# The first RMSNorm's mean square from squares of the transposed x, added on VectorE and summed by matmuls, in one encoder layer on one core

## The chip, the cores and the metric

The kernel runs on one core of a Trainium2 chip. The metric is the device time of one execution in microseconds (us), lower is better; the runs of the kernel before are summed up by their median. Engines are named as in the profile: PE is TensorE's matmul, PEld its weight load, DVE VectorE, ACT ScalarE, POOL GpSimd, SP the engine whose queue issues the loads (SPq).

## The reference, cut to what matters

One layer over x of 256 positions (T) by 2048 channels (D). Only the first lines concern the change; the rest is three branches and an MLP, all large matmuls.

```python
def rms_norm(x, g):
    y = xf * lax.rsqrt(jnp.mean(xf * xf, axis=-1, keepdims=True) + NORM_EPS)
    return y.astype(x.dtype) * g

h = rms_norm(x, norm1_g[i])
proj = h @ w_in[i]     # columns: z | xBC | dt | q | k | v | GLU | gates
dt = jax.nn.softplus(dt_raw + dt_bias)
q = rms_norm(q, q_g); k = rms_norm(k, k_g)
...
x = x + merged @ w_out[i]
x = x + relu(rms_norm(x) @ w_up)^2 @ w_down
```

## The kernel before

**Blocks and units.** All large products run as a list of blocks, each of up to 512 output columns; a block is cut into units of 256 rows of the contraction. For unit k the kernel loads a slab of weights (`raw`, line 1193, five buffers), splits it into a rounded part `hi` on ACT (line 1211) and a remainder `lo` on DVE (line 255), four buffers each, and PE does twelve (or 24 narrower) matmuls: `hi` with the activation's rounded part (1273, or 1264), `hi` with its remainder (1274, 1266), `lo` with the rounded part (1276, 1268). A block of mode "X" sums into a PSUM tile `main`, of which there are two, used in turn.

**The first blocks.** Block 0 holds the columns of dt and of the first queries (448 columns, units 0 to 7), block 1 the first keys (384 columns, units 8 to 15), block 2 the first values (384 columns, units 16 to 23). They use the unnormed x times g1 (`xgh`, `xgl`, lines 307 and 308; x is loaded transposed into four slabs `xt`, channel on the partition), and each position's factor 1/rms is multiplied in afterwards. From block 3 (unit 24, the first GLU block) on, the activation is the normed h, as `hh` and `hl`.

**The jobs around the change.** `job_rms1` finds that factor. It loads x again in natural layout (position on the partition, four `xr` of 512 KB), takes sums of squares on ACT, gets the factor per partition `r` (`st["r1"]`) from `rstd_steps`, and `spread` brings it into a row that stands on every partition, `rbc`, by a matmul of a diagonal `dg` with ones (line 296). `job_h` waits for `rbc` and makes h: sixteen `hf` on DVE (354), four `hh` on ACT (357), four `hl` on DVE (255). `job_dt` waits for `r`, reads block 0's dt columns into `dtt` (386), permutes them by matmuls (395), and computes a softplus on ACT and DVE (399 to 424), then `adt` and four matmuls with masks (436). `job_qk` (one for the queries, one for the keys) takes squares of a block on ACT (459), makes the factor `qrs` on DVE, scales into `qn` on ACT (489), marks its `main` as free, and transposes `qn` on PE (501) into `qkT` (505, 506).

**What sets the order.** Each engine works through its instructions in the order in which the Python program writes them. A planner (class `Sched`) steps the jobs, which are generators: they ask for an estimated time on an engine ("v", "a", "g", "p"), for slabs ("m"), banks ("b"), a delay ("w") or a condition ("j"), and are taken forward between units as long as the planner's credit and its own clock allow. Jobs have a priority (0 for `job_rms1` and `job_qk`, 1 for `job_h` and `job_dt`). For unit k the program writes the split of unit k + 3, then the matmuls of unit k. Where a unit needs something that no job has written yet, `require` writes the jobs' steps at once, whatever they cost: first those of priority 0, then those of 1, in the order in which they were added. The first unit of block 2 needs the PSUM tile of block 0:

```python
if u == 0:
    if bi >= 2:
        j = mains[bi - 2]
        S.require(lambda: id(j) in st["main_free"], f"block {bi - 2} read")
...
# require: while not cond(): the jobs with prio <= level, forced
for j in [x for x in self.jobs if x.prio <= level]:
    while not cond() and not j.done and self._try(j, True):
        moved = True
# job_qk of block 0, before it marks the tile as free
if off:
    yield "j", lambda: "dt_read" in st
st["main_free"].add(id(main))
```

Of the kernel before, what the change touches and what calls it, by code (L numbers as in the profile page):

```python
# [15 lines left out]
AF = mybir.ActivationFunctionType  # L16
ALU = mybir.AluOpType
AX = mybir.AxisListType
# [3 lines left out]
T = 256  # L22
D = 2048
KC = D // P
HEADS = 32
EPS = 1e-6
# [164 lines left out]
def kernel(ctx: ExitStack, tc: tile.TileContext, xT, xn, par, cm, cd, cq, w1, wq, ws, out):  # L191
    nc = tc.nc
    S = Sched()
# [11 lines left out]
    def nm(s):  # L205
        cnt[0] += 1
        return f"{s}_{cnt[0]}"

    def slab(shape, dt=F32, name="s"):
        return gp.tile([P] + list(shape), dt, tag="g", name=nm(name))  # L210

    def bank(shape=(512,), name="b"):
        return pd.tile([P] + list(shape), F32, tag="d", name=nm(name))

    def small(shape, name, dt=F32, bufs=None):
        return sm.tile([P] + list(shape), dt, tag=name, name=nm(name), bufs=bufs)

    V, A, G, PE = nc.vector, nc.scalar, nc.gpsimd, nc.tensor
# [6 lines left out]
    xt = []  # L225
# [11 lines left out]
    onesd = cp.tile([P, P], F32, name="onesd")  # L237
# [9 lines left out]
    def natural(ap):  # L247

        return ap.rearrange("p (j r) -> p r j", r=2)

    def strided(ap):
        return ap.rearrange("p (r j) -> p r j", r=2)
# [12 lines left out]
    def rstd_steps(dst, ms, n):  # L265

        s = small([n], f"rs{n}", bufs=2 if n < 64 else 1)
        r = small([n], f"rr{n}", bufs=2 if n < 64 else 1)
        yield "a", 1500 + n
        A.activation(s, ms, AF.Sqrt)  # L270
        yield "w", 1
        yield "v", (100 if n == T else 800) + 7 * n
        V.reciprocal(r, s)
        for b_ in (r, ms):
            if n == T:
                yield "v", 200 + n
            V.tensor_tensor(s, r if b_ is r else s, b_, op=ALU.mult)
        if n == T:
            yield "v", 200 + n
        V.tensor_scalar(s, s, -0.5, 1.5, op0=ALU.mult, op1=ALU.add)  # L280
        if n == T:
            yield "v", 200 + n
        V.tensor_tensor(dst, r, s, op=ALU.mult)

    def spread(r):

        yield "m", 1
        dg = slab([2, P], name="dg")
        yield "v", 400
        for t in range(2):  # L290
            V.tensor_scalar(dg[:, t, :], ID, r[:, t:t + 1], None, op0=ALU.mult)
        yield "w", 1
        yield "b", 1
        b = bank()
        yield "p", 440
        PE.matmul(b[:, :T], ones, dg, start=True, stop=True)
        S.give()
        yield "w", 1
        return b[:, :T]
# [9 lines left out]

    def job_rms1():  # L310

        xss = small([2, 2], "xss1", bufs=1)
        yield "m", 4
        xs_ = []
        for t in range(2):
            for e in range(2):
                xr = slab([1024], name="xr")
                nc.sync.dma_start(xr, xn.rearrange("(p t) d -> p t d", t=2)[:, t, e * 1024:e * 1024 + 1024])
                xs_.append(xr)
        yield "w", 2  # L320
        for t in range(2):
            for e in range(2):
                yield "a", 1300
                xr = xs_[2 * t + e]
                A.activation(xr, xr, AF.Square, accum_out=xss[:, t, e:e + 1])
        S.give(4)
        yield "w", 1
        m2 = small([2], "ms2", bufs=2)
        yield "v", 300
        V.tensor_reduce(m2, xss, axis=AX.X, op=ALU.add)  # L330
        V.tensor_scalar(m2, m2, 1.0 / D, EPS, op0=ALU.mult, op1=ALU.add)
        r2 = cp.tile([P, 2], F32, name="r2")
        yield from rstd_steps(r2, m2, 2)
        st["r1"] = r2
        b = yield from spread(r2)
        rbc = small([T], "rbc", bufs=1)
        yield "v", 400
        V.tensor_copy(natural(rbc), strided(b))
        S.banks += 1
        st["rbc1"] = rbc  # L340

    def job_h():
# [758 lines left out]
    def start_jobs():  # L1101
        S.add(job_rms1(), "rms1", 0)
# [61 lines left out]
    for o in ORDER:  # L1164
        k, i = o[0], int(o[1])
# [235 lines left out]
```

## Time and profile before

| | |
|---|---|
| median of 3 runs | 1981.73 us (1981.35 to 1984.19) |
| profiled execution, device time | 1983.86 us |
| its span, first to last instruction | 1982.1 us |
| PE busy | 1966.0 us, 99% |
| DVE busy, ACT busy, POOL busy | 1309.0, 1036.0, 47.5 us |
| read from HBM | 360.45 MB |

Start times in the rows below are microseconds from the span's start. A row of the timeline gives start, duration, engine, line, operation, output and inputs, and in brackets how long the engine had been idle and what ended that. A row of the groups gives line, engine, operation, shapes and count, then busy time and the mean ns of one. Instructions of one engine overlap a little at their ends, so that a chain of them is shorter than the sum of their durations. A matmul of plain fp32 data appears as two records.

### The profile page before, as it was taken

The numbers are of one execution on the slowest core, as the hardware profiler recorded it, in microseconds if no ns is written. First come the engines' busy times: TensorE is split into PE (matmuls) and PEld (weight loads), VectorE is DVE, ScalarE is ACT, GpSimd is POOL, SyncE is SP. The second block draws the span as 40 slices with busy tenths as digits, with TensorE's granted clock in tenths as the row PEclk, the third lists the DMA queues.
The fourth block names the chain that finished last, engine by engine and source line by source line (L and its number), as shares of the span: only waits on it lengthen the run. The fifth ranks groups of instructions, "written<-read, shape, count | busy, mean of one in ns | idle before, by whom it ended". The sixth has DMA issues, their size and how long they took to land.

```text
span 1982.1 us, 29949 instructions
## 1 busy us (share of the span) xinstructions
PE 1966.0 (99%) x11798; PEld 1766.0 (89%) x11798; DVE 1309.0 (66%) x1847; ACT 1036.0 (52%) x1446; POOL 47.5 (2%) x42
## 2 busy tenths in 40 slices
PE   8999999999999999999999999999999999999999
PEld 7999999999998888888888888999988998998887
DVE  5778887887887889896654555555555554455443
ACT  6654576777757655545654444544443443344332
POOL 0000010000000000003000000000000000000000
PEclk9999999999999999999999999999999999999999
DMA  8555554554554555555555556555555555555554
GB/s 284 184 175 183 165 185 145 167 172 144 184 170 161 176 181 178 183 191 187 190 191 183 189 189 207 194 186 192 188 190 189 189 191 191 188 186 191 190 181 149
DMA packets 105342, 364.51 MB, mean 184 GB/s; under 512 B 11760, under 2 KB 12272, under 8 KB 105200
## 3 DMA queue, kind: packets, MB, share of 16 engines
q1 hardware_dynamic: 103904, 360.23, 55.4%
q10 hardware_dynamic: 1296, 2.36, 0.3%
q8 instruction: 92, 1.51, 0.3%
q14 instruction: 50, 0.41, 0.1%
HBM read 360.45 MB, written 2.10 MB: 183 GB/s over the span
## 4 chain that ended last, share of the span: by engine, by line
PE 95%; DVE 0%; issue 0%
PE main L1273 19%; PE main L1274 19%; PE main L1276 19%; PE main L1266 11%; PE main L1264 11%; PE main L1268 11%; PE b L842 1%; PE b L864 1%; PE b L968 1%; PE b L1273 0%; PE b L1274 0%; PE b L1276 0%; PE b L819 0%; PE b L501 0%; PE b L757 0%; PE b L742 0%
## 5 line engine op out<-in xcount | busy, mean ns | idle before, releaser
L255 DVE TENSOR_TENSOR lo<-raw,hi 128x1024 fp32r<-128x1024 f32 (+2 forms) x697 | 831.5, 1194 | 643.5 <-ACT hi L1211 638.7
L1211 ACT ACTIVATE hi<-raw 128x1024 fp32r<-128x1024 f32 (+2 forms) x695 | 716.2, 1032 | 868.7 <-PE main L1274 487.8
L1273 PE MATMUL main<-hi,hh 128*128 128x512 f32 (+1 forms) x800 | 306.1, 383 | 0.0
L1274 PE MATMUL main<-hi,hl 128*128 128x512 f32 (+1 forms) x800 | 299.0, 374 | 0.0
L1266 PE MATMUL main<-x2l,hi 128*128 128x256 f32 x1024 | 246.4, 281 | 0.0
L1264 PE MATMUL main<-x2h,hi 128*128 128x256 f32 x1024 | 246.3, 279 | 0.0
L1266 PE MATMUL main<-hl,hi 128*128 128x256 f32 x896 | 216.3, 281 | 3.2 <-DVE hl L255 3.2
L1264 PE MATMUL main<-hh,hi 128*128 128x256 f32 x896 | 217.7, 282 | 0.0
L565 DVE SCALAR_TENSOR_TENSOR co<-cin,cpar,co 128x256 f32<-128x256 f32 x480 | 211.1, 491 | 0.0
L1276 PE MATMUL main<-lo,hh 128*128 128x512 f32 (+1 forms) x800 | 200.5, 372 | 0.0
L1264 PEld LDWEIGHTS main<-x2h,hi 128*128 128x128 f32 x1024 | 192.7, 188 | 0.2
L1266 PEld LDWEIGHTS main<-x2l,hi 128*128 128x128 f32 x1024 | 192.6, 188 | 0.2
L1273 PE MATMUL main<-hi,ah 128*128 128x512 f32 x480 | 188.9, 394 | 0.0
L1274 PE MATMUL main<-hi,al 128*128 128x512 f32 x480 | 188.6, 393 | 0.0
L1273 PEld LDWEIGHTS main<-hi,hh 128*128 128x128 f32 x800 | 152.5, 191 | 23.4 <-ACT hi L1211 1.2
L1274 PEld LDWEIGHTS main<-hi,hl 128*128 128x128 f32 x800 | 152.2, 190 | 22.9 <-issue 1.9
L1266 PEld LDWEIGHTS main<-hl,hi 128*128 128x128 f32 x896 | 168.8, 188 | 4.2 <-DVE hl L255 3.6
L1264 PEld LDWEIGHTS main<-hh,hi 128*128 128x128 f32 x896 | 169.2, 189 | 0.6
L1276 PEld LDWEIGHTS main<-lo,hh 128*128 128x128 f32 x800 | 148.0, 190 | 22.1
L1268 PE MATMUL main<-x2h,lo 128*128 128x256 f32 x1024 | 138.3, 277 | 0.0
L1276 PE MATMUL main<-lo,ah 128*128 128x512 f32 x480 | 130.1, 393 | 0.0
L1268 PEld LDWEIGHTS main<-x2h,lo 128*128 128x128 f32 x1024 | 127.6, 188 | 0.0
(244 smaller groups left out, 2304.5 us busy)
## 6 DMA issues: line engine op xcount, KB each, us to landing
raw<-ws_dram SPq DMA_DIRECT2D x600, 512.0 KB, 3.3
raw<-wq_dram SPq DMA_DIRECT2D x88, 384.0 KB, 3.1
raw<-w_dram SPq DMA_DIRECT2D x7, 448.0 KB, 7.0
xr<-xn_dram SPq DMA_DIRECT2D x4, 512.0 KB, 9.2
x<-xn_dram SPq DMA_DIRECT2D x4, 512.0 KB, 4.3
xt<-xT_dram SPq DMA_DIRECT2D x7, 256.0 KB, 7.0
out_dram<-x SPq DMA_DIRECT2D x4, 256.0 KB, 3.7
out_dram<-x ACTq DMA_DIRECT2D x4, 256.0 KB, 5.6
```

What stands on the lines that cost most here:

```text
L255: V.tensor_tensor(lo, raw, hi.bitcast(F32), op=ALU.subtract)
L565: V.scalar_tensor_tensor(dst[:, e, :], x[:, e, k:k + T], par_("dw", (2 * i + e) * 31 + k), dst[:, e, :], op0=ALU.mult, op1=ALU.add)
L842: PE.matmul(ba, lt, src, start=(n == 0), stop=(n == 3))
L864: PE.matmul(bd[:, i, :], em[:, 0, i, :], x[:, c, pr:pr + P], start=True, stop=True)
L968: PE.transpose(b[:, e, t * P:t * P + P], src[:, t, k * P:k * P + P], ID)
L1211: A.activation(h, r, AF.Copy)
L1264: PE.matmul(o, wh[:, e, cs], ah, start=(first and e == 0 and c % 2 == 0), stop=False, skip_group_check=True)
L1266: PE.matmul(o, wh[:, e, cs], al, start=False, stop=False, skip_group_check=True)
L1268: PE.matmul(o, wl[:, e, cs], ah, start=False, stop=(last and e == 1), skip_group_check=True)
L1273: PE.matmul(o, ah[:, xs_], wh[:, e, :], start=(first and e == 0), stop=False)
L1274: PE.matmul(o, al[:, xs_], wh[:, e, :], start=False, stop=False)
L1276: PE.matmul(o, ah[:, xs_], wl[:, e, :], start=False, stop=(last and e == 1))
```

## The change

`job_rms1` no longer loads x a second time. It squares the four slabs `xt` on ACT (into `xacc` and, three times, into one slab `xsq`), adds them on DVE (three additions of 128x1024, then one of 128x512 and one of 128x256), and sums over the partitions by matmuls with a matrix of 1/D: two of two columns, which give the mean square per partition, and one of 256 columns, which gives it as a row on every partition. Both go through `rstd_steps`, the second with 256 columns; `spread` and the copy into `rbc` fall away.

```diff
     def job_rms1():
-        xss = small([2, 2], "xss1", bufs=1)
-        yield "m", 4
...
-                nc.sync.dma_start(xr, xn.rearrange("(p t) d -> p t d", t=2)[:, t, e * 1024:e * 1024 + 1024])
...
-                yield "a", 1300
-                A.activation(xr, xr, AF.Square, accum_out=xss[:, t, e:e + 1])
+        yield "m", 2
+        acc = slab([4, T], name="xacc")
+        sq = slab([4, T], name="xsq")
+        for i in range(4):
+            yield "a", 1050
+            A.activation(sq if i else acc, xt[i], AF.Square)
+            yield "w", 1
+            if i:
+                yield "v", 1200
+                V.tensor_tensor(acc, acc, sq, op=ALU.add)
+        yield "v", 620
+        V.tensor_tensor(acc[:, 0:2, :], acc[:, 0:2, :], acc[:, 2:4, :], op=ALU.add)
+        yield "v", 350
+        V.tensor_tensor(acc[:, 0, :], acc[:, 0, :], acc[:, 1, :], op=ALU.add)
+        yield "w", 1
+        yield "b", 1
+        b = bank()
+        yield "p", 900
+        for t in range(2):
+            PE.matmul(b[:, T + 2 * t:T + 2 * t + 2], acc[:, 0, t::2], onesd[:, 0:2], start=True, stop=True)
+        PE.matmul(b[:, :T], onesd, acc[:, 0, :], start=True, stop=True)
...
-        b = yield from spread(r2)
         rbc = small([T], "rbc", bufs=1)
-        V.tensor_copy(natural(rbc), strided(b))
-        S.banks += 1
+        yield from rstd_steps(rbc, ms, T)
         st["rbc1"] = rbc
```

Since the jobs are planned, the order moves beyond these lines. Lines of the changed kernel that stand behind this function are six higher (501 becomes 507, 395 becomes 401, 436 becomes 442, 354 becomes 360, 386 becomes 392). In the rows that follow a name's number is that of one allocation.

On PE, the matmuls of `job_rms1`. Before, `spread` and the four matmuls of `job_dt` stand together behind unit 10 (three units into block 1):

```order
L1276 MATMUL main_360<-lo_326,xgh_99 128x384 x4
L296 MATMUL b_430<-dg_405,ones 128x256
L395 MATMUL b_436<-dtt_342,perm_343 128x128 x4
L1273 MATMUL main_360<-hi_356,xgh_99 128x384
L1274 MATMUL main_360<-hi_356,xgl_103 128x384
```

In the changed kernel the sums stand one unit earlier, behind unit 9:

```order
L1282 MATMUL main_357<-lo_302,xgh_98 128x384 x4
L331 MATMUL b_400<-onesd,xacc_253 128x2 x2
L332 MATMUL b_400<-xacc_253,onesd 128x256
L1279 MATMUL main_357<-hi_321,xgh_99 128x384
L1280 MATMUL main_357<-hi_321,xgl_103 128x384
```

The matmuls of `job_dt` have left this place.

On PE, the step from block 1 (unit 15) to block 2 (unit 16). Before, nothing stands between them:

```order
L1273 MATMUL main_360<-hi_473,xgh_101 128x384
L1274 MATMUL main_360<-hi_473,xgl_105 128x384
L1276 MATMUL main_360<-lo_474,xgh_101 128x384 x4
L1273 MATMUL main_581<-hi_499,xgh_98 128x384
L1274 MATMUL main_581<-hi_499,xgl_102 128x384
```

In the changed kernel:

```order
L1280 MATMUL main_357<-hi_459,xgl_105 128x384
L1282 MATMUL main_357<-lo_460,xgh_101 128x384 x4
L507 MATMUL b_599<-cmask,qn_591 128x128 x4
L507 MATMUL b_600<-cmask,qn_591 128x128 x2
L401 MATMUL b_644<-dtt_339,perm_340 128x128 x4
L442 MATMUL b_673<-adt,cmask 128x128 x4
L1279 MATMUL main_684<-hi_478,xgh_98 128x384
```

The transposes of the keys, the permutation of dt and the products of `adt` now stand ahead of block 2's first matmul.

On DVE, around the splits of units 18 to 20 (`lo_556`, `lo_578`, `lo_608` before). Before, jobs and splits alternate:

```order
L255 TENSOR_TENSOR lo_556<-raw_497,hi_555 128x768
L354 SCALAR_TENSOR_TENSOR hf_521<-xt_86,cpar,rbc_459 128x256 x2
L399 TENSOR_TENSOR dtt_342<-b_436,cpar 128x128
L255 TENSOR_TENSOR lo_578<-raw_524,hi_577 128x768
L255 TENSOR_TENSOR lo_608<-raw_553,hi_607 128x768
L469 TENSOR_TENSOR r1sq_604<-r_376 128x2
```

In the changed kernel 40 rows stand between the split of unit 19 (`lo_548`) and that of unit 20 (`lo_700`): the factors of queries and keys, all the rest of `job_h`, then all of `job_dt`. Twelve of them, where h passes over into dt:

```order
L360 SCALAR_TENSOR_TENSOR hf_516<-xt_85,cpar,rbc_453 128x256 x3
L360 SCALAR_TENSOR_TENSOR hf_613<-xt_86,cpar,rbc_453 128x256 x4
L255 TENSOR_TENSOR hl_518<-hf_516,hh_517 128x1024
L360 SCALAR_TENSOR_TENSOR hf_622<-xt_87,cpar,rbc_453 128x256 x4
L255 TENSOR_TENSOR hl_615<-hf_613,hh_614 128x1024
L360 SCALAR_TENSOR_TENSOR hf_631<-xt_88,cpar,rbc_453 128x256 x4
L255 TENSOR_TENSOR hl_624<-hf_622,hh_623 128x1024
L255 TENSOR_TENSOR hl_633<-hf_631,hh_632 128x1024
L392 TENSOR_SCALAR dtt_339<-main_169,r_426 128x64 x2
L393 MEMSET dtt_339 128x64
L405 TENSOR_TENSOR dtt_339<-b_644,cpar 128x128
L414 TENSOR_SCALAR dtt_339<-dtt_339 128x128
```

ACT has the matching run between its splits of the same two units: twelve `qn`, six squares, four `hh`, and the table load and activations of the softplus. No other place of the program has such a run on these engines. On SP only the four loads of `xr` are gone; the loads of weights keep their order.

More of the change, by code (lines that the diff above doesn't have):

```diff
@@ L310, in job_rms1 @@
     def job_rms1():
-        xss = small([2, 2], "xss1", bufs=1)
-        yield "m", 4
-        xs_ = []
-        for t in range(2):
-            for e in range(2):
-                xr = slab([1024], name="xr")
-                nc.sync.dma_start(xr, xn.rearrange("(p t) d -> p t d", t=2)[:, t, e * 1024:e * 1024 + 1024])
[L319 to L322, printed above, removed]
-                yield "a", 1300
-                xr = xs_[2 * t + e]
-                A.activation(xr, xr, AF.Square, accum_out=xss[:, t, e:e + 1])
-        S.give(4)
+        yield "m", 2
[16 more added lines that the diff above has]
+        yield "p", 900
+        for t in range(2):
+            PE.matmul(b[:, T + 2 * t:T + 2 * t + 2], acc[:, 0, t::2], onesd[:, 0:2], start=True, stop=True)
+        PE.matmul(b[:, :T], onesd, acc[:, 0, :], start=True, stop=True)
+        S.give(2)
         yield "w", 1
         m2 = small([2], "ms2", bufs=2)
-        yield "v", 300
-        V.tensor_reduce(m2, xss, axis=AX.X, op=ALU.add)
-        V.tensor_scalar(m2, m2, 1.0 / D, EPS, op0=ALU.mult, op1=ALU.add)
+        ms = small([T], "ms256", bufs=1)
+        yield "v", 600
+        V.tensor_scalar(m2, b[:, T:T + 4:2], 1.0, EPS, op0=ALU.mult, op1=ALU.add)
+        V.tensor_scalar(ms, b[:, :T], 1.0, EPS, op0=ALU.mult, op1=ALU.add)
+        S.banks += 1
         r2 = cp.tile([P, 2], F32, name="r2")
@@ L334, in job_rms1 @@
         st["r1"] = r2
-        b = yield from spread(r2)
         rbc = small([T], "rbc", bufs=1)
-        yield "v", 400
-        V.tensor_copy(natural(rbc), strided(b))
-        S.banks += 1
+        yield from rstd_steps(rbc, ms, T)
         st["rbc1"] = rbc
```

## The prediction, made before the changed kernel ran

> **What bounds the kernel now.** I read the page's first lines, then who waited for whom on PE, then the timeline of the first 95 us.
>
> ```profile
> span 1982.1 us, 29949 instructions
> PE 1966.0 (99%) x11798; PEld 1766.0 (89%) x11798; DVE 1309.0 (66%) x1847; ACT 1036.0 (52%) x1446; POOL 47.5 (2%) x42
> ```
>
> PE is idle for 16.1 us of the span. So a microsecond comes off only where PE waits today, and any new wait of PE is added in full: there is no later slack to take it up. All waits of PE that the profile shows, with the times they occur and the longest:
>
> ```profile
> PE b L296 <- DVE dg L291: 4.1, 1, 4.1
> PE main L1266 <- DVE hl L255: 3.2, 2, 2.2
> PE main L1273 <- ACT hi L1211: 2.9, 2, 2.1
> ```
>
> The first and the 2.1 of the third lie in block 1, the second in the first GLU block. PE's rows there (first matmul of units 8, 9, 11, 12 and 16, and what stands between):
>
> ```profile
> 28.31 0.34 PE L1273 MATMUL main<-hi,xgh 128*128 128x384 f32 x1
> ...
> 32.65 0.45 PE L1273 MATMUL main<-hi,xgh 128*128 128x384 f32 x1 [2.09 <-ACT hi L1211]
> ...
> 41.22 1.14 PE L296 MATMUL b<-dg,ones 128*128 128x256 f32 x2 [4.09 <-DVE dg L291]
> 42.16 1.91 PE L395 MATMUL b<-dtt,perm 128*128 128x128 f32 x8
> 43.73 0.67 PE L1273 MATMUL main<-hi,xgh 128*128 128x384 f32 x1
> ...
> 46.38 0.34 PE L1273 MATMUL main<-hi,xgh 128*128 128x384 f32 x1
> ...
> 54.79 0.45 PE L1273 MATMUL main<-hi,xgh 128*128 128x384 f32 x1
> ...
> 61.19 0.82 PE L501 MATMUL b<-cmask,qn 128*128 128x128 f32 x6
> ```
>
> A unit of 384 columns takes (54.79 - 46.38) / 4 = 2.10 us; the one behind the 4.1 us stop took 46.38 - 43.73 = 2.65. Six transposes (501) take PE 0.58 (61.19 to 61.77, where the next unit starts).
>
> **What goes.** The four `xr` loads go, 2 MB. Unit 9's split waited for its weights:
>
> ```profile
> 31.75 0.84 ACT L1211 ACTIVATE hi<-raw 128x768 fp32r<-128x768 f32 x1 [3.16 <-DMA raw<-wq_dram]
> ...
> 36.58 0.96 DVE L255 TENSOR_TENSOR lo<-raw,hi 128x768 fp32r<-128x768 f32 x1 [1.15 <-ACT hi L1211]
> ```
>
> (The second row is the split of unit 11, used below.) Without 2 MB ahead of it in the queue unit 9's wait is gone, and with it PE's 2.1. The spread (296) and its 4.1 us wait go too; PE's L395 moves.
>
> **First new wait: the sum behind unit 9.** Before, ACT reached the end of unit 8's split at 21.11 + 1.67 = 22.78:
>
> ```profile
> 21.11 1.67 ACT L1211 ACTIVATE hi<-raw 128x896 fp32r<-128x896 f32 x2
> 23.75 1.06 ACT L325 ACTIVATE xr<-xr 128x1024 f32<-128x1024 f32 x1 [0.97 <-DMA xr<-xn_dram]
> ...
> L255 DVE TENSOR_TENSOR hl<-hf,hh 128x1024 fp32r<-128x1024 f32 x4 | 4.8, 1220 | 0.0
> ...
> 946.20 0.42 DVE L277 TENSOR_TENSOR rs<-rr 128x256 f32<-128x256 f32 x1
> ```
>
> Now two squares stand ahead of it, 1.06 each like L325: 24.9. The rest goes hand over hand, since `xsq` is one slab: each square waits for the addition before it. `lo` of unit 8 25.8; first addition, priced by the subtraction of the same size (1.22), 27.0; square 28.0 and unit 9's `hi` 28.8, `lo` 29.7; second addition 30.9; square 31.9, `hi` 32.7, `lo` 33.6; third addition 34.8; the 128x512 addition lies between the rows of 0.42 and 1.22, I take 0.7: 35.5; a `lo` 36.4; the last addition 0.42: 36.8. PE is through with unit 9 at 28.31 + 2 x 2.10 = 32.5, and L331 stands next: it waits 4.3 us, much as L296 did. Bounds: 3 to 5.5. L331 is four records of 2 columns; nothing like it is in the trace; L395's at this clock took 0.24 each, so 0 to 1.0 in all, and I take 1.0, its weights being as wide. L332 is L296's 1.14. So unit 10 starts at 38.9, ends 41.6 if it is slowed like unit 11, and unit 15 ends at 41.6 + 5 x 2.10 = 52.1. The 256-column steps on DVE are covered here by splits that stand three units ahead.
>
> How much the stop costs beyond its length is read from the clock:
>
> ```profile
> 40.00:50.00 10.00, 8.78 (x43) 8.60 (x44) 7.42 (x22) 4.88 (x15) 0.00 (x0) 0.83 0.54 162
> ```
>
> The granted clock was 0.83 in the stretch behind the 4.1 us stop, and unit 11 lost 0.55. [...] I go by the row.
>
> **Second new wait: between units 15 and 16.** This decides. PE must run L507 (keys), L401 and L442 before block 2, and it doesn't pass over a waiting matmul: from 41.22 it ran L296 and L395 first, though unit 11's weights were split by 36.58 + 0.96 = 37.54. L442 needs `adt`, the end of `job_dt`, which on DVE stands behind all of `job_h`, which stands behind the keys' factor. Rows for the steps:
>
> ```profile
> 45.30 1.28 DVE L354 SCALAR_TENSOR_TENSOR hf<-xt,cpar,rbc 128x256 f32<-128x256 f32 x3
> ...
> 52.35 1.40 ACT L489 ACTIVATE qn<-main,qrs 128x128 f32<-128x128 f32 x5 [1.30 <-DVE qrs L482]
> ...
> 55.33 0.31 ACT L459 ACTIVATE junk<-main 128x128 f32<-128x128 f32 x1
> ...
> 57.53 0.19 ACT L459 ACTIVATION_READ_ACCUMULATOR junk<-main 128x1 f32 x1
> ...
> 62.00 0.18 DVE L273 RECIPROCAL rr<-rs 128x6 f32<-128x6 f32 x1
> ...
> 63.03 0.36 DVE L482 TENSOR_SCALAR qrs<-qrs,r 128x3 f32<-128x3 f32 x2
> ...
> 64.79 0.69 ACT L505 ACTIVATE qkT<-b,qgs 128x512 f32<-128x512 f32 x1
> 65.36 0.49 ACT L506 ACTIVATE qkT<-b,qgs 128x256 f32<-128x256 f32 x1
> ...
> L357 ACT ACTIVATE hh<-hf 128x1024 fp32r<-128x1024 f32 x4 | 4.3, 1064 | 0.0
> ```
>
> From PE's end of unit 15, 52.1: ACT can write unit 19's `hi` only then (its buffer is unit 15's), 52.9, DVE's `lo` 54.4 behind one `hf`. The queries' factor 1.4 (62.00 to 63.39): 55.8. Six `qn` 1.6: 57.4. Six squares of the keys 2.4 (55.33 to 57.72): 59.8. The keys' factor, 0.6 for its inputs and root (three instructions of some 0.2, as at 62.00), then 1.4: 61.8. Six `qn` 1.6: 63.3, and PE's transposes end at 63.7. Meanwhile DVE does 3 + 4 `hf` at 0.42, to 64.7. ACT's copies of `qkT` (1.06 by the two rows, the first begun before the last transposes) end at 64.5, the first `hh` at 65.5. Then DVE is the chain: `hl` 1.2, four `hf` 1.7, `hl` 1.2, four `hf` 1.7, `hl` 1.2, `hl` 1.2, 8.2 in all: 73.7. Now dt:
>
> ```profile
> 41.08 0.47 DVE L386 TENSOR_SCALAR dtt<-main,r 128x64 f32<-128x64 f32 x2
> ...
> 69.09 0.35 ACT L403 ACTIVATE dtt<-dtt 128x128 f32<-128x128 f32 x1
> ...
> 70.76 0.31 ACT L404 ACTIVATE dtt<-dtt 128x128 f32<-128x128 f32 x1
> ...
> 75.66 0.22 DVE L408 TENSOR_SCALAR dtt<-dtt 128x128 f32<-128x128 f32 x1
> ...
> 77.23 0.29 DVE L411 TENSOR_TENSOR dtt<-dtt 128x128 f32<-128x128 f32 x1
> ...
> 83.56 0.22 DVE L413 TENSOR_SCALAR dtt<-dtt 128x128 f32<-128x128 f32 x1
> 83.82 1.27 DVE L415 SCALAR_TENSOR_TENSOR dtt<-dtt 128x128 f32<-128x128 f32 x4
> ...
> 86.14 1.27 DVE L418 SCALAR_TENSOR_TENSOR dtt<-dtt 128x128 f32<-128x128 f32 x4
> ...
> 94.08 0.28 DVE L420 SCALAR_TENSOR_TENSOR dtt<-dtt 128x128 f32<-128x128 f32 x1
> ...
> 94.99 0.36 DVE L424 SCALAR_TENSOR_TENSOR adt<-dt,ea 128x64 f32<-128x64 f32 x2
> ```
>
> Reading dt 0.5: 74.2. L401 on a PE that has stood, as L395 stood, 1.9: 76.1. DVE's addition of the bias, 0.3: 76.4. ACT's absolute value, table load and exponential, 69.09 to 71.07, 2.0: 78.4. DVE's softplus 1.9 + 1.5 + 1.3 + 1.3 (the four stretches of the rows) = 6.0: 84.4. L442, eight records like L395, 1.9: unit 16 starts at 86.3. It started at 54.79: 31.5 us later. PE's idle part is about 52.1 to 84.4 less 2.5 of small matmuls, near 30.
>
> **What comes back.** Work that stood behind unit 16 before is now ahead of it: six transposes, 0.58, and L436, here on a warm clock:
>
> ```profile
> 106.87 0.89 PE b L436 x8
> ```
>
> H is complete, so the 3.2 us wait in the GLU block goes. Against that, unit 16 runs slowed, 0.6. After it four units are split already (8 us of PE), in which ACT and DVE split on; I cost that at nothing, and if the cover failed it would be a split, 2 us. The 2 MB, the SP queue's four issues and the lighter DVE behind unit 24 bring nothing, PE being full.
>
> Sum: 31.5 + 0.6 - 0.6 - 0.9 - 3.2 = +27.4. Against the profiled execution (span 1982.1, device time 1983.86, 2.1 above the median but within the runs shown) that is a span near 2009.5; against the median, 1981.73 + 27.4 = 2009.
>
> **Rivals.** (a) Faster: PE isn't held at unit 16, either because it takes ready matmuls past L507 or because the chain is done by then. Units 16 to 19 are split and would cover 8.4 us. Then 2.1, 4.1 and 3.2 go and 4.3 comes: 1981.7 - 5 = 1977. It decides if `adt` were written by 52.1; the row at 41.22 and DVE's order speak against it. 2 in 100. (b) Only the keys' part holds PE: dt's read slips in early, and PE goes on at 63.7, 22.6 earlier: 1981.7 + 4.8 = 1986.5. It needs L392 ahead of `hl_633`; the order has it behind. 4 in 100. (c) Longer: each hand-over between engines (some fifteen in the chain) costs 0.2 more than the rows' small gaps, 3 us, and the slowed clock lasts through block 2 as in unit 11, 8 x 0.55 = 4.4: 2016.5. Long idle behind single bursts speaks for it, that units 12 to 15 were back at 2.10 against. 8 in 100.
>
> **How the numbers follow.** The forecast has the remaining 86 in 100. Within it the first wait may be 1.3 shorter or 1.2 longer, L331 and the clock 2.6 cheaper, the chain from 52.1 to 84.4 ten per cent either way (3.2) where ACT and DVE overlap otherwise than I laid them: 2003 to 2015. A measurement of this kernel tells some 0.2%, 4 us, from no change. (a) is the only case below that (0.24%), (b) ends just above it, so half of it counts as no change: faster 0.02, same 0.02, slower 0.96.
>
> **What would show it.** Right: PE's waits list two large ones in 28 to 90 us, on L331 for `xacc` (about 4) and, in pieces, on L507, L401 and L442 (about 30 together, the last behind `adt`); unit 16 near 86; a granted clock below 1 behind them; no 3.2 for `hl`; PE busy about as before. Wrong: unit 16 before 75, or a wait of PE behind 100 us.

## The result and the profile after

The changed kernel takes 2014.24 us (median of 4 runs, 2013.32 to 2014.64) against 1981.68 (4 runs, 1981.35 to 1984.19): the ratio is 1.0161, 95% interval 1.0143 to 1.0178. The profiled execution took 2013.32 us, with a span of 2011.5. Its page begins:

```profile
span 2011.5 us, 29964 instructions
PE 1971.6 (98%) x11802; PEld 1770.2 (88%) x11802; DVE 1317.5 (65%) x1854; ACT 1037.8 (52%) x1443; POOL 44.0 (2%) x42
```

PE is busy 5.6 us longer than before (1966.0), and idle for 39.9 us of the span instead of 16.1. The waits of PE, largest first (total, times, longest):

```profile
PE b L401 <- issue: 10.0, 1, 10.0
PE b L507 <- ACT qn L495: 9.4, 2, 9.1
PE b L442 <- DVE adt L430: 8.6, 1, 8.6
PE b L331 <- DVE xacc L325: 4.4, 1, 4.4
PE main L1279 <- ACT hi L1217: 1.6, 1, 1.6
```

The two waits of before on `dg` (4.1) and `hl` (3.2) are gone. Four new ones of 32.4 us stand in their place, and three of them, 28.0 us, lie in one hole. PE's timeline from unit 8 to unit 17 (first matmul of units 8, 10, 11, 16 and 17, and what stands between):

```profile
27.48 0.34 PE L1279 MATMUL main<-hi,xgh 128*128 128x384 f32 x1
...
36.20 0.63 PE L331 MATMUL b<-onesd,xacc 128*128 128x2 f32 x4 [4.37 <-DVE xacc L325]
36.69 0.94 PE L332 MATMUL b<-xacc,onesd 128*128 128x256 f32 x2
37.07 0.88 PE L1279 MATMUL main<-hi,xgh 128*128 128x384 f32 x1
...
40.88 0.34 PE L1279 MATMUL main<-hi,xgh 128*128 128x384 f32 x1
...
60.59 0.47 PE L507 MATMUL b<-cmask,qn 128*128 128x128 f32 x1 [9.09 <-ACT qn L495]
...
72.71 2.04 PE L401 MATMUL b<-dtt,perm 128*128 128x128 f32 x8 [10.01 <-issue]
83.34 2.05 PE L442 MATMUL b<-adt,cmask 128*128 128x128 f32 x8 [8.59 <-DVE adt L430]
85.04 0.67 PE L1279 MATMUL main<-hi,xgh 128*128 128x384 f32 x1
...
88.66 0.34 PE L1279 MATMUL main<-hi,xgh 128*128 128x384 f32 x1
```

Unit 16 starts at 85.04 instead of 54.79. What PE waited for is the chain on ACT and DVE (the first addition and the square that had to wait for it, then the last `hl`, dt's read and `adt`):

```profile
24.91 1.22 DVE L321 TENSOR_TENSOR xacc<-xacc,xsq 128x1024 f32<-128x1024 f32 x1
26.22 1.06 ACT L317 ACTIVATE xsq<-xt 128x1024 f32<-128x1024 f32 x1 [2.22 <-DVE xacc L321]
...
69.78 2.44 DVE L255 TENSOR_TENSOR hl<-hf,hh 128x1024 fp32r<-128x1024 f32 x2
72.13 0.47 DVE L392 TENSOR_SCALAR dtt<-main,r 128x64 f32<-128x64 f32 x2
...
82.83 0.36 DVE L430 SCALAR_TENSOR_TENSOR adt<-dt,ea 128x64 f32<-128x64 f32 x2
```

The wait on L401 that the profile puts down to "issue" is the wait for dt's read: L392 ends at 72.60, and L401 starts at 72.71 at the end of DVE's memset of the same tile (72.57 to 72.68). The page can't name a releaser there, the order can.

The hole by ten microseconds (busy times of PE, PEld, DVE, ACT, POOL, then the granted clock, the DMA share and GB/s):

```profile
60.00:70.00 10.00, 1.80 (x6) 1.11 (x6) 8.70 (x20) 5.76 (x12) 0.00 (x0) 0.50 0.00 0
70.00:80.00 10.00, 2.04 (x8) 1.78 (x8) 5.66 (x14) 3.01 (x5) 0.00 (x0) 0.50 0.00 0
80.00:90.00 10.00, 6.66 (x28) 6.69 (x29) 4.44 (x15) 1.62 (x6) 0.00 (x0) 0.59 0.01 2
```

DVE is the busiest engine in the first two stretches, PE runs at half clock until unit 16 is under way (0.50 up to 88.18), and even the loads stop: their queue (SPq) waits 36.2 us for the subtraction (L255) that frees the next weight buffer.

### The profile page after: what moved, and what is told of

The parts are those of the page before. It is cut to its first block, busy times and chain, and to the rows that moved or that the text cites. A ratio compares the mean times of both kernels' runs of the same rounds, so it can differ in the third digit from the quotient of the medians.

```text
span 2011.5 us, 29964 instructions
## 1 busy us (share of the span) xinstructions
PE 1971.6 (98%) x11802; PEld 1770.2 (88%) x11802; DVE 1317.5 (65%) x1854; ACT 1037.8 (52%) x1443; POOL 44.0 (2%) x42
## 4 chain that ended last, share of the span: by engine, by line
PE 98%; issue 1%; DVE 1%; ACT 0%; DMA 0%; SPq 0%; DVEq 0%
PE main L1280 20%; PE main L1279 20%; PE main L1282 19%; PE main L1272 11%; PE main L1270 11%; PE main L1274 11%; PE b L848 1%; PE b L870 1%; PE b L974 1%; PE b L1279 0%; PE b L1280 0%; PE b L1282 0%; PE b L825 0%; DMA raw<-w_dram 0%; PE b L507 0%
## 5 line engine op out<-in xcount | busy, mean ns | idle before, releaser
L255 DVE TENSOR_TENSOR lo<-raw,hi 128x1024 fp32r<-128x1024 f32 (+2 forms) x697 | 832.9, 1196 | 654.4 <-ACT hi L1217 651.6
```

The lines of the kernel that those rows point to most:

```text
L255: V.tensor_tensor(lo, raw, hi.bitcast(F32), op=ALU.subtract)
```

## The experiments

Theory A is the prediction's: the time is one of order. Because the new factor is planned so much longer on VectorE, dt's read isn't written before block 2 needs the tile, and the planner then writes the keys' factor, all of `job_h` and all of `job_dt` at once, ahead of block 2. The open points were which part of the change causes that, what each wait is worth, and where some 2 us beyond the waits came from. Each kernel's profile is summed up by three numbers: the first matmul on `hh` (block 3), the first on `x2h` (start of the MLP), and the time from there to the first matmul of the last block's `b`:

| kernel | median us | first hh | first x2h | x2h to last b |
|---|---|---|---|---|
| before (first profile) | 1981.68 | 72.89 | 1264.11 | 691.4 |
| changed (first profile) | 2014.24 | 103.99 | 1291.60 | 693.2 |
| changed again | 2013.84 | 105.08 | 1292.69 | 693.2 |
| dt's read first | 1998.19 | 78.50 | 1279.25 | 690.5 |
| short softplus | 2010.32 | 100.15 | 1287.76 | 693.2 |
| three slabs | 2007.96 | 98.01 | 1282.41 | 697.0 |
| before again | 1983.41 | 70.72 | 1263.45 | 691.4 |
| one load | 1983.14 | 66.17 | 1258.66 | 695.1 |
| spread | 1987.96 | 70.96 | 1261.93 | 695.9 |
| spread, three slabs | 1980.41 | 64.14 | 1257.37 | 693.0 |
| one load, four slabs | 1979.35 | 67.65 | 1260.37 | 691.4 |
| before, other places | 1986.14 | 70.87 | 1262.30 | 695.7 |
| spread, three slabs, other places | 1984.44 | 64.22 | 1259.82 | 696.2 |

The kernel before ran beside each group: 1983.93 for the first four experiments, 1983.77 for the next four, 1983.69 for the last three.

**The changed kernel again.** No edit.

> The changed kernel as it is, with the kernel before on the same chip. Two readings of the 33 us are tested. Theory A: PE waits for a chain that the planner wrote ahead of block 2 (waits on L331, L507, L401 and L442, 32.4 us in the first profile), and all else is as it was; the profile should again show unit 16 at 85 +- 0.5 and these waits at 32 +- 1. The difference of the two profiles had 3.4 us that are not in the first 300 us: the MLP, from its first matmul on x2h to its last block, took 693.2 in the changed kernel and 691.4 before, without any wait of PE. Theory A1: that is the spread of one execution against another; in this execution the stretch lies anywhere from 691 to 694. Theory A2: the changed kernel's PE is slower there for good; the stretch is 693.2 +- 0.3 again.

Measured: 2013.84 (2012.74 to 2014.38), ratio 1.0150 (1.0136 to 1.0163). The waits are 10.0, 9.4 and 8.6 again, that on `xacc` 4.8, and the MLP takes 693.2 again. Unit 16 starts at 85.67, 0.2 us past the range that I gave. The hole is the same from run to run; so is the slower MLP.

**Dt's read as a job of its own.** The read of block 0's dt columns is taken out of `job_dt` and given priority 0, ahead of the queries' job:

```diff
+    def job_dtread(main):
+        yield "j", lambda: "r1" in st
...
+        st["dt_read"] = True
-            return ([(job_dt(m), 1)] if j == 0 else []) + ...
+            return ([(job_dtread(m), 0), (job_dt(m), 1)] if j == 0 else []) + ...
```

> The changed kernel with all its new work, but the reading of dt's columns out of block 0's tile is a job of its own with priority 0, so that the tile is free in time and nothing is written at once ahead of block 2. Theory A (the order is the cause, not the work): the waits on L507, L401 and L442 go, the one on L331 stays at 4.4; unit 16 starts at 53 to 57 and the time is 1981 to 1990. Rival B (the added work on VectorE is the cause, the 256-column root above all): the same work still holds the chain that frees the tile, and the time stays above 2000.

Measured: 1998.19 (1996.81 to 1999.23), ratio 1.0071 (1.0059 to 1.0084). The waits on L507, L401 and L442 are gone, as Theory A has it, and the time is 15.65 us under the changed kernel's beside it; but it is 8 us above the range that I gave. PE's timeline shows where they went, unit 16 and the first GLU block:

```profile
58.33 0.69 PE L1287 MATMUL main<-hi,xgh 128*128 128x384 f32 x1 [4.95 <-ACT qn L503]
...
82.75 0.38 PE L1280 MATMUL main<-hl,hi 128*128 128x256 f32 x1 [3.88 <-DVE hl L255]
...
93.07 0.39 PE L1280 MATMUL main<-hl,hi 128*128 128x256 f32 x1 [2.86 <-DVE hl L255]
...
103.50 0.41 PE L1280 MATMUL main<-hl,hi 128*128 128x256 f32 x1 [2.91 <-DVE hl L255]
...
104.13 0.41 PE L1278 MATMUL main<-hh,hi 128*128 128x256 f32 x1
```

Unit 16 still waits for the queries' scaling, and h is late in its turn: 9.7 us on `hl`, where the kernel before had 3.2. In the changed kernel h is complete before block 2, so that these waits were hidden in the hole. The edit shows that the forced rows are the hole; it doesn't undo what makes h late.

**A shorter softplus.** Eight of the polynomial's steps on DVE are left out:

```diff
-        for n in (8, 7, 6, 5):
-            V.scalar_tensor_tensor(q, q, 1.0 / (2 * n + 1), z2, op0=ALU.add, op1=ALU.mult)
...
-        for n in (4, 3, 2, 1):
-            V.scalar_tensor_tensor(q, q, 1.0 / (2 * n + 1), z2, op0=ALU.add, op1=ALU.mult)
```

> The changed kernel without eight of the nine steps of the softplus polynomial in dt (left out: lines 421 and 424 of the changed kernel; the planner's requests stay, so the order stays). Eight steps at 0.325 us each stand in the chain that ends with adt. Theory A: PE's wait on L442 is shorter by 2.6, unit 16 starts at 82.4 instead of 85.0, and the time is 2.6 +- 0.7 below the changed kernel's on this chip. Rival C (the end of the wait is set by ACT, by PE's clock or by weights, and the length of the DVE chain has room): within 0.5 of the changed kernel.

Measured: 2010.32 (2009.49 to 2011.0), 3.5 us less than the changed kernel beside it, 0.2 more than the range I gave; ratio to before 1.0134 (1.0120 to 1.0148). The last wait of the hole:

```profile
80.09 2.05 PE L438 MATMUL b<-adt,cmask 128*128 128x128 f32 x8 [5.98 <-DVE adt L426]
```

It fell from 8.59 to 5.98, by 2.6 us, what the two rows L415 and L418 of before promise (1.27 twice). A step of the softplus is on the path, microsecond for microsecond. What is gained beyond it lies in no edited step: in the profiles (3.8 us apart) this kernel is 0.6 us earlier at the end of unit 10, and another 0.6 comes in unit 16, where the half clock lasts 1.8 us here (81.79 to 83.62) and 3.1 in the changed kernel (85.04 to 88.18).

**Three slabs for the squares.** A square no longer waits for the addition that reads the slab before it:

```diff
-        sq = slab([4, T], name="xsq")
+        sqs = [slab([4, T], name="xsq") for _ in range(3)]
...
-            A.activation(sq if i else acc, xt[i], AF.Square)
+            A.activation(sqs[i - 1] if i else acc, xt[i], AF.Square)
```

> The changed kernel with three slabs for the squares instead of one, so that a square no longer waits for the addition before it. Theory A: the hand over hand of ACT and DVE sets the wait on L331; it falls from 4.4 to between 0 and 1.5, the slowed matmuls behind it go, all that follows moves up with it, and the time is 4 to 6 below the changed kernel's. Rival D (the additions on DVE with the splits between them are the chain, so that ACT's waiting costs nothing): the wait stays above 3 and the time within 1.5.

Measured: 2007.96 (2007.2 to 2008.1), 5.9 us less than the changed kernel; ratio to before 1.0121 (1.0107 to 1.0135). PE's row for the sum and the waits:

```profile
32.02 0.63 PE L331 MATMUL b<-onesd,xacc 128*128 128x2 f32 x4 [0.18 <-DVE xacc L325]
```

```profile
PE b L401 <- issue: 10.0, 1, 10.0
PE b L507 <- ACT qn L495: 9.4, 2, 9.1
PE b L442 <- DVE adt L430: 8.6, 1, 8.6
```

The wait on `xacc` was the taking of turns on one slab, and it is apart from the hole: with the sum 4.2 us earlier the hole is as long as ever. The first matmul on `hh` is 6.0 us earlier than in the first profile of the changed kernel (4.2 of wait, the rest the slowed unit behind it). From there to `x2h` it takes 3.2 us less than the changed kernel, with the same instructions in the same order, and then its MLP takes 697.0, 3.8 us more. That was a surprise, and the next seven experiments deal with it and with the cause of the hole.

**The kernel before again.** No edit; a second profile.

> The kernel before, unchanged, for a second profile of it on the chip of the next three. What is open: from the first block on x2h (1264.1 in the first profile of before) to the first row of the last block's b (1955.5) PE shows no wait, yet the changed kernel took 693.2 us there in two profiles, against 691.4. Theory A1 (PE's pace in the MLP differs a little from run to run by itself, so what lay beyond the waits in the result, some 2 to 4 us, isn't the change's): this profile's stretch lies anywhere from 690 to 697. Theory A2 (the slower pace belongs to the changed kernel): 691.4 within 0.3 again. Median 1981 to 1985 either way.

Measured: 1983.41 (1981.49 to 1984.65, 11 runs), ratio 0.9998 (0.9989 to 1.0007). The MLP takes 691.4, to a tenth. Theory A1, a pace that wanders from run to run, falls: the pace belongs to the program.

**One load of x.** In the kernel before, three of four loads in natural layout go:

```diff
-                xr = slab([1024], name="xr")
-                nc.sync.dma_start(xr, ...)
+                xr = slab([1024], name="xr") if not xs_ else xs_[0]
+                if not xs_:
+                    nc.sync.dma_start(xr, ...)
```

> The kernel before with one of the four loads of x in natural layout kept; its slab is squared four times, so that three quarters of x's mean square are left out and every instruction but three loads stays. This prices what the change gains by itself: 1.5 MB less ahead of unit 9's weights. Theory A: unit 9's wait of 2.1 goes, the squares no longer wait for DMAs, so the factor is there sooner and the 4.1 us wait on the spread gets shorter by up to 2; nothing else. 3 to 4 us under before, 1977.5 to 1981. Rival B (PE is bound by the rate of the weights' loads in this stretch, the loads' time goes in full: 1.5 MB at the 160 to 200 GB/s of the stretch, 8 to 9 us): near 1974. Rival C (the next weights are as late): within 1 us of before.

Measured: 1983.14 (1981.49 to 1983.82), ratio 0.9998 (0.9990 to 1.0007): no change, as in Rival C, where Theory A had 3 to 4 us less. But Rival C's reason doesn't hold, since the early gain is there. PE's row of the spread:

```profile
34.73 0.70 PE L296 MATMUL b<-dg,ones 128*128 128x256 f32 x2 [0.90 <-DVE dg L291]
```

It was at 39.07 in the second profile of before, with a wait of 4.08. The first matmul on `hh` is 4.6 us earlier, that on `x2h` 4.8, and then the MLP takes 695.1 and gives 3.7 of it back.

**The spread in place of the 256-column root.** In the changed kernel the third product, its eps and its root go, and the row is made as before:

```diff
-        PE.matmul(b[:, :T], onesd, acc[:, 0, :], start=True, stop=True)
...
-        V.tensor_scalar(ms, b[:, :T], 1.0, EPS, op0=ALU.mult, op1=ALU.add)
...
+        b = yield from spread(r2)
...
-        yield from rstd_steps(rbc, ms, T)
+        yield "v", 400
+        V.tensor_copy(natural(rbc), strided(b))
```

> The changed kernel with the 256-column mean square (the sum of 256 columns on PE, its eps, and its root with 256 columns on DVE) put back to the spread of before: dg, a matmul with ones, and a copy into rbc. The squares, their additions and the two small sums stay, and the loads stay away. Theory A (the lump between units 15 and 16 comes of the 256-column root alone: its planned 1892 ns and four more steps on VectorE use up the credit that dt's read needs): no waits on L507, L401 and L442 there, unit 16 within 62, the wait on the sums for xacc stays at 4 to 5; the time is 26 to 32 us under the changed kernel, 1981 to 1987. Rival B (the lump comes of the additions on VectorE, or of the sum's late end): the waits stay, at more than half their 28 us, and the time is above 1998. Rival C (as in the experiment with dt's read first, the late factor comes out as waits on hl behind 80 us): 1988 to 1998, with 6 us or more on hl.

Measured: 1987.96 (1985.06 to 1988.56), ratio to before 1.0019 (1.0010 to 1.0028), 4.2 us over before beside it, where the changed kernel was 29.9 over. All waits of PE over 1.6 us:

```profile
PE b L331 <- DVE xacc L325: 4.4, 1, 4.4
PE main L1272 <- DVE hl L255: 4.1, 3, 2.6
PE main L1279 <- DVE cin L543: 1.9, 1, 1.9
```

No hole, and the first matmul on `hh` at 70.96, 0.24 from before's 70.72. So the 256-column mean square with its root makes the hole; the squares, their five additions on DVE and the sum's late end don't. The run takes out the root's instructions and the time planned for them together. That it is the planned time is read from the planner, which charges a job what it asks for; no run shows it by itself. The time is 1 us above the range that I gave; the MLP's 695.9, 4.4 us over before's, is more than that.

**The spread and three slabs.** The two edits together.

> The same, and with three slabs xsq instead of one, so that squares and additions needn't take turns. Theory A: both costs are gone, the wait on xacc falls from 4 to 5 to under 1, what stays is the gain of the loads that went: 1976 to 1981, so faster than the kernel before by 2 to 6 us. Rival B (the three slabs are missing elsewhere, or the slower pace behind them, 697 in the MLP as in the run with three slabs, comes with them): 1981 to 1985, with a wait on xacc under 1 all the same. Rival C (waits on hl in the first GLU block take it back): 1982 to 1988.

Measured: 1980.41 (1978.61 to 1982.42), ratio 0.9985 (0.9976 to 0.9994). The waits:

```profile
PE main L1272 <- DVE hl L255: 4.0, 3, 2.6
PE main L1279 <- DVE cin L543: 1.9, 1, 1.9
PE main L1279 <- ACT hi L1214: 1.6, 1, 1.6
```

None on `xacc`; `hh` 6.6 us and `x2h` 6.1 us earlier than in before, and the MLP 1.6 longer. This is the fastest kernel of the study that computes the whole layer, 3.4 us under before, so the idea of the change can win a little once its two costs are out.

**One load, four slabs.** The MLP's pace followed neither the start time nor the waits. What else differs is where the tiles lie. The compiled program of the kernel with one load has `x2h` at addresses 38336, 46656, 100736 and 59136, before has 38336, 54976, 121536 and 71616: dropping three slabs moves later ones. Here three loads fetch 16 columns each, so that all four slabs are taken and every tile lies where before has it:

```diff
-                nc.sync.dma_start(xr, ...[:, t, e * 1024:e * 1024 + 1024])
+                w = 1024 if len(xs_) == 3 else 16
+                nc.sync.dma_start(xr[:, :w], ...[:, t, e * 1024:e * 1024 + w])
...
-                A.activation(xr, xr, AF.Square, accum_out=xss[:, t, e:e + 1])
+                A.activation(xr, xs_[3], AF.Square, accum_out=xss[:, t, e:e + 1])
```

> As in the experiment with one load, but with all four slabs xr in use, so that every tile lies where it lies in the kernel before: three of the four loads fetch 16 columns instead of 1024, and the four squares all read the one slab that is loaded whole (three quarters of x's mean square are left out again). Open is why the kernel with one load had its MLP block x2h 4.8 us earlier (1258.66 against 1263.45) and yet took 695.1 us from there to the last b, against 691.4. Theory P (place: PE's pace in the MLP goes by where the tiles lie in memory, and one slab in place of four had moved them): 691.4 again, the 4.8 us stay, and the time is 4 to 5 us under before: 1977 to 1980. Theory T (time: an earlier arrival is taken back later by something that is late anyway): near 695, the time within 1.5 us of before.

Measured: 1979.35 (1977.93 to 1980.13), ratio 0.9978 (0.9970 to 0.9987). The first matmul on `x2h` and the first of the last `b`, in the second profile of before, with one load, and with one load and four slabs:

```profile
1263.45 0.28 PE L1264 MATMUL main<-x2h,hi 128*128 128x256 f32 x1
...
1954.88 0.40 PE L1273 MATMUL b<-hi,ah 128*128 128x512 f32 x1
```

```profile
1258.66 0.28 PE L1265 MATMUL main<-x2h,hi 128*128 128x256 f32 x1
...
1953.74 0.39 PE L1274 MATMUL b<-hi,ah 128*128 128x512 f32 x1
```

```profile
1260.37 0.28 PE L1265 MATMUL main<-x2h,hi 128*128 128x256 f32 x1
...
1951.80 0.41 PE L1274 MATMUL b<-hi,ah 128*128 128x512 f32 x1
```

691.4, 695.1 and 691.4: with before's places before's pace is back, though PE arrives 3.1 us earlier (not the 4.8 that I expected: the wait on the spread is 2.25 us here), and the gain of the loads stays to the end. Theory P holds, Theory T falls.

**Before, other places.** The reverse: no work and no order of the kernel changed, three one-column memsets on GpSimd take a slab each at the start.

```diff
+    for _ in range(3):
+        G.memset(slab([1], name="spare"), 0.0)
```

> The kernel before with three spare slabs taken at the start (one column each set to zero by GpSimd), which shifts which slab goes where for all that follows, and changes no order and no work. Theory P: the first 100 us and x2h's start as in before (1263.5 within 1.5), but the MLP takes another time than 691.4, somewhere from 688 to 698, and the median moves by as much. Theory T: 691.4 again, median within 1 us of before.

Measured: 1986.14 (1984.12 to 1987.36), ratio 1.0017 (1.0008 to 1.0026). Its waits on `dg` (4.1) and `hl` (3.3) are before's. The same two rows:

```profile
1262.30 0.28 PE L1266 MATMUL main<-x2h,hi 128*128 128x256 f32 x1
...
1957.96 0.39 PE L1275 MATMUL b<-hi,ah 128*128 128x512 f32 x1
```

695.7 instead of 691.4, by nothing but the places: in the compiled program PE, ACT and DVE have before's instructions in before's order. The median moved by 2.4 us and not by the 4.3 of the MLP, where I expected as much; `x2h` came 1.2 us earlier, which takes back a part.

**The spread, three slabs, other places.** Two such memsets ahead of the fastest kernel.

> The kernel with the spread and three slabs xsq, with two spare slabs taken at the start in the same way. Theory P: waits as without them (hl about 4, cin 1.9), x2h near 1257.4, the MLP other than 693.0, from 688 to 698, so a time from 1975 to 1985. Theory T: 693.0 and 1980.4 again, within 1.

Measured: 1984.44 (1982.61 to 1985.77), ratio 1.0003 (0.9994 to 1.0012). The first matmul on `hh` is where it was (64.22 against 64.14), `x2h` 2.4 us later (1259.82 against 1257.37, outside what I expected), the MLP 3.2 longer. Of the 2.4, some 1.5 are the clock's and not the places': both kernels wait 2.6 us on `hl` up to 73.8, and behind it the granted clock was 0.50 from 74.23 to 77.65 in this profile, 1.00 in the other, and the first product of queries and keys came at 81.01 instead of 79.39. The remaining 0.9 and the 3.2 make 4.1, and the medians are 4.0 apart. So a program's luck with its places is worth 4 us here, more than the 3.4 that the fastest kernel wins. That it is faster than before is measured; that its design is, and not its places, is not.

## Why the prediction was right, and where it was off

**The hole (+31.5).** Unit 16 was put at 86.3 and came at 85.04, 30.25 later than before. Along the chain: PE through with unit 15 at 60.59 - 9.09 = 51.5 (52.1 predicted); the keys' transposes done at 62.7, which is 61.37 + 1.33 (63.7); the last `hl` at 69.78 + 2.44 = 72.2 (73.7); `adt` at 82.83 + 0.36 = 83.2 (84.4). Every step came a little early, none in another order. The wait on L442 shrinking by just the removed DVE work, and the hole vanishing both with dt's read first and with the spread, are the causal tests.

**The first wait (4.3).** 4.37, by taking turns on one slab: with three slabs 0.18. L331 and L332 cost PE 0.87 (36.20 to 37.07), not the 2.1 that I allowed. Unit 10 behind them cost more: 3.81 us (37.07 to 40.88) instead of 2.65. The sum of the two was right by chance.

**What comes back.** The 3.2 us wait on `hl` went, as said, and so did unit 9's of 2.1. Unit 16 ran slowed by 88.66 - 85.04 - 2.10 = 1.5 us, not 0.6, at a granted clock of 0.57 in that stretch. The small matmuls inside the hole don't bring the clock back: 0.50 throughout.

**The sum.** At the first matmul on `hh` the shift was 31.1 where my terms give 31.5; at `x2h` it was 27.5 against 27.4. Since with three slabs the stretch from `hh` to `x2h` is 3.2 us shorter in the same order of instructions, that last agreement is better than the method deserves. So is the range: its terms reach up to 2009 + 1.2 + 3.2 = 2013.4, and only the rounding to 2015 takes in the measured 2014.24.

**What was missed.** The median lies 5.1 us above 1981.73 + 27.4. Of these, 2.1 is the choice of base: the sum was made against a profile of 1983.86 and then added to the median of three runs; beside it on one chip the kernel before takes 1983.93, and the distance is 29.9. Another 0.9 is the changed kernel's profile below its own median. The rest, 2.1, is in the step "PE being full": I took PE's pace outside the waits as fixed. It isn't; 1.8 us are the MLP's 693.2 against 691.4, and the runs show that this goes by where the tiles lie. In the kernel before, the three spare slabs alone cost PE 4.3 us in the MLP (695.7 against 691.4); what in the placement does it stays open.

**The clock.** I went by the row of the one stop of 4.1 us, and so counted a stop of 4.3 us as slowed. It was slowed in all eight profiles with a stop of 4.1 to 5.0 us. Behind it the granted clock was 0.83 in the kernel before (40 to 50 us) and 0.79 in before with other places (38 to 46), 0.64 in the changed kernel (36.2 to 41), 0.66 in its second profile and with dt's read first, and 0.83 with the short softplus (34 to 44 each). The range of my sum has 2.6 us for "L331 and the clock": 1.0 is L331, and the other 1.6 is for a stop that isn't slowed. No run shows such a stop of this length; in the changed kernel unit 10 behind it took 3.81 us, 1.7 over the 2.10 of a unit. The rows of the experiment with dt's read first, shown above, go further: the `hl` wait of 2.91 us, shorter than the 3.41 us for which the clock then stays low, was followed by matmuls of 256 columns of 0.41 us instead of 0.28. In the traces the falls of the clock came behind stretches of 3.41 us in which PE was busy for 0 to 1.41 us, most of them not idle throughout (the last section has the rows); why it falls there is not shown.

**The rivals.** (a) and (b) are out. The hand-overs of (c) were no longer than the rows; its slow clock lasted for one unit, not for the block.

## What to carry to other kernels

Where a planner spends credit per engine, the cost of an added instruction is not its duration (here 3.7 us of 256-column steps on DVE, which no matmul waited for), but what it pushes past the point at which something is forced: read the order at the next forced step before you add up durations. With PE busy for 99% of the span such steps turned into time here (28.0 us of waits in the hole), and work that "moves" into the hole must be found again when the hole is closed, as the waits on `hl` were. The tiles' places alone moved the time by 2.4 us here (1986.14 against 1983.69) and the MLP by 4.3 (695.7 against 691.4); try an edit in a second placement before you credit it.

## What the hardware showed unexpectedly

- PE's pace in the MLP, without any wait and at a granted clock of 1.00, went by where the tiles lie: the same MLP took 691.4 us in the kernel before and 695.7 with three spare slabs ahead of it, and 690.5 to 697.0 over all kernels. Programs with equal addresses agreed to 0.1 us (691.4 three times, 693.2 three times), although they came to it up to 5 us apart.
- No run moved a single tile, so what makes a place slow is not shown. A lead, from the addresses in nine of the compiled programs and the matmuls' starts in their traces: the MLP's matmuls with `x2h` or `x2l` start 115.7 ns apart on average where the activation's address lies 192 bytes past that of the weights modulo 256, and 117.9 to 118.6 ns apart in the three other cases; in the kernel before alone it is 115.5 against 117.1 to 118.9. The kernel before has two thirds of them in the fast case, with three spare slabs it has one third. The lead isn't whole: in the changed kernel another case was faster still (113.3 against 115.2).
- The clock fell also where PE hadn't stood still for the 3.41 us that it then stayed low. In the 13 profiles, from 30 us to the end of the last block's work, it stays at 0.50 for 3.41 us or a multiple of it, so I counted windows of that length from each profile's own changes of the clock. PE was busy for 0 to 1.41 us in each of the 21 windows there that a fall followed, and wholly idle in only three; in the windows at full clock that none followed it was busy for 1.55 us or more. In the kernel before PE was busy for 0.11 us ahead of the fall (37.92 to 41.33), in the changed kernel for 0.78 and 0.88 us ahead of the two (33.56 to 36.98, 50.63 to 54.04), and for 1.68 us in a window there that none followed (30.15 to 33.56). The same wait was slowed in one profile and not in another, as it fell in these windows; what sets the windows is not shown. Both profiles of the kernel before wait 2.2 us on `hl` (up to 89.73 in the first and 87.55 in the second). The window around the wait and the next one, in the first and in the second:

```profile
85.70:89.12 3.42, 1.86 (x13) 1.55 (x12) 3.32 (x7) 1.07 (x2) 0.00 (x0) 1.00 0.47 163
89.12:92.53 3.41, 2.80 (x23) 2.80 (x24) 1.69 (x2) 0.68 (x1) 0.00 (x0) 1.00 0.48 156
```

```profile
84.14:87.55 3.41, 1.26 (x10) 1.01 (x8) 3.31 (x7) 0.47 (x1) 0.00 (x0) 1.00 0.57 169
87.55:90.97 3.42, 3.42 (x16) 3.42 (x17) 1.08 (x1) 0.00 (x0) 0.00 (x0) 0.50 0.37 139
```

PE was busy for 1.86 us in the one and 1.26 in the other, and the granted clock behind it was 1.00 and 0.50.

- The slowing came after 2.25 us on the spread in the run with one load and four slabs, where small matmuls followed. After 0.90 us in the same place it did not come:

```profile
36.16 0.70 PE L296 MATMUL b<-dg,ones 128*128 128x256 f32 x2 [2.25 <-DVE dg L291]
36.70 1.11 PE L396 MATMUL b<-dtt,perm 128*128 128x128 f32 x8
37.51 0.63 PE L1274 MATMUL main<-hi,xgh 128*128 128x384 f32 x1
37.94 0.52 PE L1275 MATMUL main<-hi,xgl 128*128 128x384 f32 x1
```

```profile
36.08 0.43 PE L1274 MATMUL main<-hi,xgh 128*128 128x384 f32 x1
36.34 0.34 PE L1275 MATMUL main<-hi,xgl 128*128 128x384 f32 x1
```

The first fence is the timeline with four slabs, the second with one: 0.52 against 0.34 for a matmul of 384 columns.
